# The first heads of a hybrid mLSTM and band-attention trunk: a pool of their own, and their 57 modulation columns dealt anew

## The chip, the cores and the metric

The kernel runs on one core of a Trainium2 chip. The metric is the device time of one launch in microseconds (us), as the median of several runs. TensorE (PE) multiplies, with its weight loads shown apart as PEld; VectorE (DVE) and ScalarE (ACT) work element by element; GpSimd (POOL) and SyncE (SP) only issue DMAs here.

## What is computed

Two layers work on a sequence of 512 tokens of width 2048. The first is an mLSTM layer with 8 heads, the second a band-attention layer whose keys and values come from the residual stream between the two. Each is a modulated RMSNorm, a mixer, and a gated residual. This study is about the first layer:

```python
mod = sc @ ada_w[l] + ada_b[l]                     # sc = silu(c): 1 x 2048 times 2048 x 6144
shift, scale, gate = ...                           # three rows of 2048
h = modulate(rmsnorm(x, g_pre[l]), shift, scale)
proj = h @ w_in                                    # queries, keys, values, output gates o, branch z, cell gates
qk = silu(causal_conv(proj[..., :A_V0], conv_w, conv_b))
ht = mlstm_chunkwise(q, k, v, log_i, log_f)        # per head: decayed scores times values
y = sigmoid(o) * rmsnorm_per_head(ht) * silu(z)
x = x + gate * rmsnorm(y @ w_out)
```

The second layer does the same with `band_attention_mixer`, and its keys and values are modulated by two further rows (`kv_ada_w`). All inputs and outputs are float32.

## The kernel before

**Products.** A float32 product is made of three: each operand is split into a high part (an ACT cast) and a low part (a DVE subtraction), and PE adds high x high, high x low and low x high (`mm3`). A weight piece `wr` of up to 128x1024 is loaded by SP, cast by ACT and subtracted by DVE (L243) into `wh`, which PE then reads. Three `wr` and three `wh` buffers turn round, so the piece numbered n can't be cast before PE has done with n-3, and can't be loaded before n-3 has been subtracted.

**Columns.** The modulation rows are made without PE: for every 128 of their elements a 128x2048 block `ada` (1024 KB) is loaded and one DVE instruction (L552) multiplies it by silu(c) and sums it into one column of `mod`. Here such a block is called a column. The 32 columns of shift and scale (numbers 0 to 31) are needed at the start, two for each of the 16 input tiles. The others are background work: 57 of them (numbers 32 to 47, 96 to 127 and 48 to 56) are summed by `background(n)`, which sums up to n columns that are loaded and asks POOL for new ones. Three are under way at a time, in two buffers of the pool `ada` and one of `ada1`. An `ada` load waits for the sum that last read its buffer. `paced` orders a sum behind the PE product written before it, which places it but is no wait.

**Stages.** At the start, 41 steps (`first_steps`) go over the 16 input tiles: a step (k,) makes the input tile `h1_k` (DVE L521, ACT L523, DVE L524) and multiplies it with six weight tiles into the six accumulators `ps_lead`; the other steps multiply finished input tiles with the other fourteen weight tiles of head 0 and head 1's queries and keys (`ps_l`), and DVE adds these parts in SBUF (L731). Pieces 0 to 40 are their weights. Then heads follow one after the other:

- Head 0 has its projections but for the values from the start. `conv` turns queries and keys into the convolved `qk` tiles (ACT, three DVE taps at L797, ACT SiLU, split). The cell gates follow (`gates`), a chain of DVE, ACT and PE steps with rows that go to DRAM and come back to all partitions as `nm`; DVE adds the causal mask to it (`nmd`, L956). Then the values `ps_v` (pieces 41 to 48), the scores `ps_s`, and decayed scores times values (`ps_n`).
- Head 1 has its queries and keys from the start too; pieces 49 to 56 are its values, 57 to 72 its `o` and `z`.
- Head 2 (`HALF`) is whole, with pieces from 73. From its `o` and `z` on, and in all later heads, products go in the form with seven products in place of eight, and the background must be over.

The normalisation of a head is made of two rows (`row_out`): sums over partitions, by PE with a matrix of ones (`ps_d`, `ps_q`), go through ACT into a tile `row` and by a POOL DMA to DRAM. `factor` brings them back on 16 partitions, DVE and ACT make one factor per token, and POOL brings it to all partitions (`ssum`). POOL's queue is in order: a load of a row that waits for its store holds the column loads behind it.

**The pool t1.** Three buffers of 128x512 (tag `t`) serve nearly everything short-lived: normalised input, convolution accumulators `cv`, copies `cu` of interleaved rows, decays `e`, `sz`, squares `sq`, and the norm rows. A tile must wait until the third last tile of that pool has been read for the last time.

**Order.** The program is written in the order above; a scheduler at build time orders each engine's instructions by its own estimate of durations, with priorities (`tc.high_priority`), and `pin` keeps those marked in program order.

Of the kernel before, what the change touches and what calls it, by code (L numbers as in the profile page):

```python
# [15 lines left out]
P = 128  # L16
# [171 lines left out]
def hybrid_trunk(ctx, tc, xT, xN, c, adaT, cols, wst, wg, ext, kc, out):  # L188
# [132 lines left out]

    def proj(mat, xs, pss, nk, k0, k1, last, t0=0, t1=S, first=None):

        g = len(pss)
        for ka in range(k0, k1, nk):
            [(hi, lo)] = wpiece(mat)
            for k in range(ka, ka + nk):
                x = xs(k) if callable(xs) else xs[k]
                for i, ps in enumerate(pss):
                    w = slice(((k - ka) * g + i) * P, ((k - ka) * g + i + 1) * P)  # L330
                    mm3(ps, hi[:, w], lo[:, w], x[:, 0, t0:t1], x[:, 1, t0:t1], k == (k0 if first is None else first), k == last, S)

    def proj_a(mat, xs, ps, t0=0, t1=S):
        proj(mat, xs, [ps], 8, 0, len(xs), len(xs) - 1, t0, t1)

# [339 lines left out]
    pending = [2 * KT + i for i in range(KT)] + [96 + i for i in range(32)] + [48 + i for i in range(SHIFTS)]  # L675
    loaded = []

# [5 lines left out]
    def background(n):  # L683

        for a in loaded[:n]:
            ada_sum(*a, paced)
        del loaded[:n]
        while pending and len(loaded) < 3:
            p, bufs = (bp, 1) if len(pending) % 3 == 1 else (ap_, 2)
            loaded.append(ada_load(pending.pop(0), p, bufs, pin, queue=nc.gpsimd))  # L690

    due = []
    for n, step in enumerate(steps):
        if n > len(steps) - 6:
            background(2 if n % 2 else 0)
# [36 lines left out]
    st.close()  # L732
    ahead[0] = AHEAD

    hp = hst.enter_context(pool("head"))
# [11 lines left out]
    def gates():  # L747
        g_ps = newa("ps_g")
        for k in range(KT):
            for i in range(2):  # L750
                mm(bank(g_ps[:32], S), gw[:, k, :], walk(h1[k][:, i, :], S), k == 0 and i == 0, k == KT - 1 and i == 1)
        g32 = tp.tile([P, S], F32, tag="t", name="g32")
        nc.scalar.copy(like(g32[:32], S), read(g_ps[:32], S))
# [32 lines left out]

    def conv(ps, ch, name, lead, woven):

        acc = tp.tile([P, S], F32, tag="t", name=f"cv_{name}")
        with tc.high_priority(lead):  # L790
            if woven:
                rows = tp.tile([P, S], F32, tag="t", name=f"cu_{name}")
                nc.scalar.copy(like(rows, S), read(ps, S))
                ps = rows
# [88 lines left out]
    def row_out(h, i, ps, f):  # L883

        r = tp.tile([P, S], F32, tag="t", name=f"row{h}_{i}")[0:1]
        nc.scalar.activation(like(r, S), read(ps[0:1], S), f)
        nc.gpsimd.dma_start(dsc[h, i : i + 1], r)
# [33 lines left out]
    for h in range(NH):  # L921
# [4 lines left out]
        for i in range(4):  # L926
            if h > HALF:
                if i % 2 == 0:
                    zs = pair((i // 2) * (V0 // 2) + h * DK, f"zq{h}_{i}", BANKS[i // 2], HEAD_PAIRS, {1: head_due} if i else {}, lead=AHEAD - 30 * i)
                ps = zs[i % 2]  # L930
            elif h < 2:
                ps = (lead, qk1)[h][i]
            else:
                ps = newp(f"ps_qk{h}_{i}")
                proj_a("a_w_in", h1, ps)
            qk.append(conv(ps, chs[i], f"{h}_{i}", AHEAD if h == HALF else 100 if h > HALF and i > 1 else 0, h in (0, HALF)))
            if 1 < h <= HALF:
                background(2)
                if i in (2, 3):
                    head_due()  # L940
# [7 lines left out]
        if h == 0:  # L948
            background(2)
            gates()  # L950
# [48 lines left out]
        if h < HALF:  # L999
            background(2 + (h == 0))  # L1000
        if h:
            so = []
        for i in range(4):
# [7 lines left out]
            elif h:  # L1011
                ps = newp(f"ps_o{h}_{i}")
                proj_a("a_w_in", h1, ps)
                so.append(acp.tile([P, S], F32, tag="so", name=f"so{h}_{i}", bufs=6))
                nc.scalar.activation(like(so[i], S), read(ps, S), AF.Sigmoid)
                background(2)
        for i in range(4):
            if h >= HALF:
                break
            if h:  # L1020
                ps = newp(f"ps_z{h}_{i}")
                proj_a("a_w_in", h1, ps)
            else:
# [4 lines left out]
            if h and i < 3:  # L1028
                background(2)
        if h == 0:  # L1030
            background(2)
        if h == NH - 1:
# [36 lines left out]
        if h < HALF:  # L1069
            background(3)  # L1070
        if h == 3:
# [637 lines left out]
```

## Time and profile before

| what | value |
|---|---|
| median of 3 runs | 2637.78 us (2635.75 to 2638.52) |
| profiled execution | 2635.22 us |
| its span in the profile | 2633.4 us |
| PE busy | 2574.4 us (98%), 17994 products |
| DVE busy | 2335.1 us (89%) |
| DMA, share of 16 engines, 300 to 400 us | 0.84 |

The views that the prediction shows are these. The waits view gives for an engine and line: who was waited for, the us in total, how often, and the longest. The timeline gives start us, duration us, engine, line, operation, out<-in, shape, how many, and in brackets the idle time before with what ended it. A window row gives, for a stretch, the busy us of PE, PEld, DVE, ACT and POOL with instruction counts, the granted PE clock, the share of the DMA engines and GB/s. A DMA row gives the issues of a line in a stretch, the KB of each, and the median us from issue to landing. Neighbouring rows of one engine overlap a little, so a duration in a row is taken from start to start.

### The profile page before, as it was taken

How to read it: one execution, taken by the hardware profiler on the slowest of the kernel's cores; microseconds unless marked ns; L12 is line 12 of the kernel's file. 1: busy time of each engine (PE TensorE's matmuls, PEld its weight loads, DVE VectorE, ACT ScalarE, POOL GpSimd, SP SyncE). 2: the span in 40 equal slices, each digit the busy share in tenths (PEclk: the TensorE clock that was granted, in tenths of full speed). 3: DMA queues.
4: the chain of work that ended last, by engine and by line, in shares of the span. 5: the costliest groups of instructions: out<-in, count | busy, mean ns of one | idle time of the engine just before them, and what ended most of it. 6: DMA issues, size and time to landing. Idle time of an engine off the chain costs nothing.

```text
span 2633.4 us, 45758 instructions
## 1 busy us (share of the span) xinstructions
PE 2574.4 (98%) x17994; PEld 2407.5 (91%) x17994; DVE 2335.1 (89%) x3812; ACT 1428.7 (54%) x2106; POOL 59.8 (2%) x118
## 2 busy tenths in 40 slices
PE   8999999999999999999999999999999999999998
PEld 6887787899999999999999898788999899999887
DVE  8978988999989999899998886977997999999767
ACT  4344533466555665556655453578543766776523
POOL 0000111000000000000000000000000000000000
PEclk9999999999999999999999999999999999999999
DMA  9876787533333333333336548988654544444787
GB/s 364 313 265 251 272 329 290 192 108 114 124 102 129 115 111 125 105 125 118 110 130 237 195 150 327 301 259 302 226 179 146 171 130 138 138 130 132 254 299 251
DMA packets 155315, 510.62 MB, mean 194 GB/s; under 512 B 17893, under 2 KB 31749, under 8 KB 140633
## 3 DMA queue, kind: packets, MB, share of 16 engines
q1 hardware_dynamic: 144346, 443.89, 49.6%
q0 software_dynamic: 10752, 63.79, 6.6%
q8 instruction: 141, 2.31, 0.4%
q14 instruction: 76, 0.62, 0.1%
HBM read 473.96 MB, written 38.90 MB: 195 GB/s over the span
## 4 chain that ended last, share of the span: by engine, by line
PE 56%; DVE 25%; DMA 8%; issue 7%; ACT 3%; POOL 0%; SPq 0%; DVEq 0%; ACTq 0%; POOLq 0%
DVE wh L243 6%; PE ps_y L311 5%; PE ps_azo L311 4%; PE ps_czo L311 4%; PE ps_dzo L311 4%; DVE ada L552 3%; PE ps_y_True L311 3%; PE ps_dz L311 3%; PE ps_cz L311 3%; PE ps_y_False L311 3%; PE ps_az L311 3%; DMA wr<-in_wst 3%; DVE wsh L243 2%; PE ps_bzo L311 2%; DVE cv L797 2%
## 5 line engine op out<-in xcount | busy, mean ns | idle before, releaser
L243 ACT CAST wh<-wr 128x1024 fp32r<-128x1024 f32 (+1 forms) x536 | 553.3, 1034 | 473.3 <-DVE wr L283 102.0
L243 DVE TENSOR_TENSOR wh<-wr,wh 128x1024 fp32r<-128x1024 f32 (+1 forms) x536 | 643.3, 1203 | 127.2 <-ACT wh L243 126.3
L243 ACT CAST wsh<-ws 128x768 fp32r<-128x768 f32 (+1 forms) x296 | 241.8, 817 | 298.4 <-PE ps_az L311 67.1
L243 DVE TENSOR_TENSOR wsh<-ws,wsh 128x768 fp32r<-128x768 f32 (+1 forms) x296 | 276.8, 935 | 45.7 <-ACT wsh L243 44.5
L552 DVE CUSTOM_DVE_ANT_0 ada<-ada,scB,cl 128x2048 f32<-128x2048 f32 (+1 forms) x89 | 205.8, 2322 | 11.3 <-DMA ada<-in_adaT 11.2
L282 DVE TENSOR_TENSOR ws<-wr 128x512 f32<-128x512 f32 (+1 forms) x296 | 198.5, 673 | 5.3 <-DMA wr<-in_wst 5.0
L311 PE MATMUL ps_y_False<-wh,y 128*128 128x512 f32 x768 | 168.6, 380 | 2.3 <-DVE wh L243 2.2
L311 PE MATMUL ps_y<-wh,y 128*128 128x512 f32 x768 | 168.6, 380 | 0.1
L311 PEld LDWEIGHTS ps_y_False<-wh,y 128*128 128x128 f32 x768 | 144.3, 189 | 24.4 <-DVE wh L243 4.2
L311 PEld LDWEIGHTS ps_y<-wh,y 128*128 128x128 f32 x768 | 144.3, 189 | 20.8 <-DVE wh L243 0.5
L311 PE MATMUL ps_kv<-wh,hkv 128*128 128x512 f32 x576 | 127.3, 381 | 1.6 <-DVE wh L243 1.5
L311 PE MATMUL ps_v<-wh,h 128*128 128x512 f32 x576 | 127.3, 380 | 0.0
L311 PEld LDWEIGHTS ps_kv<-wh,hkv 128*128 128x128 f32 x576 | 108.0, 189 | 18.5 <-DVE wh L243 3.3
L284 DVE TENSOR_TENSOR ws<-wr 128x256 f32<-128x256 f32 (+1 forms) x296 | 122.1, 414 | 3.1
L283 DVE TENSOR_TENSOR wr<-ws,wr 128x256 f32<-128x256 f32 (+1 forms) x296 | 121.8, 413 | 2.4
L311 PEld LDWEIGHTS ps_v<-wh,h 128*128 128x128 f32 x576 | 108.3, 189 | 15.8 <-issue 0.9
L311 PE MATMUL ps_l<-h,wh 128*128 128x512 f32 x480 | 107.7, 380 | 2.1 <-DVE wh L243 2.1
L311 PEld LDWEIGHTS ps_l<-h,wh 128*128 128x128 f32 x480 | 90.3, 189 | 16.5 <-DVE wh L243 3.3
L311 PE MATMUL ps_azo<-h,wh 128*128 128x256 f32 (+1 forms) x606 | 92.9, 285 | 0.0
L311 PE MATMUL ps_y_True<-wh,y 128*128 128x512 f32 x384 | 83.3, 379 | 0.0
L311 PEld LDWEIGHTS ps_y_True<-wh,y 128*128 128x128 f32 x384 | 72.5, 189 | 10.2
L311 PEld LDWEIGHTS ps_azo<-h,wh 128*128 128x128 f32 x606 | 79.2, 192 | 1.1
(431 smaller groups left out, 5825.2 us busy)
## 6 DMA issues: line engine op xcount, KB each, us to landing
wr<-in_wst SPq DMA_DIRECT2D x506, 512.0 KB, 3.7
ada<-in_adaT POOLq DMA_DIRECT2D x57, 1024.0 KB, 7.1
ada<-in_adaT SPq DMA_DIRECT2D x49, 1024.0 KB, 7.0
ada<-in_adaT SPq DMA_DIRECT2D x36, 512.0 KB, 6.5
wr<-in_wst SPq DMA_DIRECT2D x26, 384.0 KB, 6.2
xt<-nsc SPq DMA_DIRECT2D x32, 256.0 KB, 3.8
yr<-ysc SPq DMA_DIRECT2D x28, 256.0 KB, 5.4
ysc<-zo SPq DMA_DIRECT2D x24, 256.0 KB, 3.9
```

The lines of the kernel that those rows point to most:

```text
L243: ins = nc.scalar.copy(hi, src), nc.vector.tensor_tensor(lo, src, hi.bitcast(F32), op=ALU.subtract)
L282: nc.vector.tensor_tensor(t[:, : 2 * w], r[:, w : 3 * w], r[:, : 2 * w], op=ALU.subtract)
L283: nc.vector.tensor_tensor(r[:, w : 2 * w], t[:, w : 2 * w], r[:, :w], op=ALU.add)
L284: nc.vector.tensor_tensor(t[:, 2 * w :], r[:, 3 * w :], r[:, w : 2 * w], op=ALU.subtract)
L311: product[0] = nc.tensor.matmul(ps, a, b, start=start, stop=stop)
L552: pin(nc.vector.tensor_tensor_reduce(c, c, (sc or scB)[:, j * w : (j + 1) * w], 1.0, mod[:, i : i + 1] if j else col(CB + i), ALU.mult, AL ...
L797: nc.vector.scalar_tensor_tensor(acc[:, d:], ps[:, : S - d], col(CW + 32 * (3 - d) + ch), acc[:, d:], op0=ALU.mult, op1=ALU.add)
```

## The change

- A new pool `t0` beside `t1`: convolution accumulators of heads 0 to 2 (three buffers), copies and the gates' `g32` (two), norm rows of heads 0 and 1 (two). It also holds a fourth buffer for columns, from the end of the start on.
- The 57 background columns are dealt anew: summing begins 13 steps before the end of the start in place of 5; after that fewer are asked for at each place, and places in the middle of the projections of head 1 and head 2 are added (`mid`).
- Head 0's mask addition is written behind its values in place of ahead of them.
- The copies of the attention bias (`bsc`, two per head, DRAM to DRAM by SP) move from all eight heads to heads 3 to 7.

```diff
-    def proj(mat, xs, pss, nk, k0, k1, last, t0=0, t1=S, first=None):
+    def proj(mat, xs, pss, nk, k0, k1, last, t0=0, t1=S, first=None, mid=None):
         for ka in range(k0, k1, nk):
+            if mid and ka > k0:
+                mid()
...
-    loaded = []
+    loaded, ring = [], [(ap_, 2), (ap_, 2), (bp, 1)]
...
-        while pending and len(loaded) < 3:
-            p, bufs = (bp, 1) if len(pending) % 3 == 1 else (ap_, 2)
+        while pending and len(loaded) < len(ring):
+            p, bufs = ring.pop(0)
+            ring.append((p, bufs))
...
-        if n > len(steps) - 6:
+        if n > len(steps) - 14:
             background(2 if n % 2 else 0)
...
+    ep = mst.enter_context(pool("t0", side="right"))
+    ring.insert(0, (ep, 1))
...
+    def early_tile(h, tag, bufs, name):
+        return ep.tile([P, S], F32, tag=tag, name=name, bufs=bufs) if h else tp.tile([P, S], F32, tag="t", name=name)
...
-        acc = tp.tile([P, S], F32, tag="t", name=f"cv_{name}")
+        acc = early_tile(early, "cv", 3, f"cv_{name}")
-                rows = tp.tile([P, S], F32, tag="t", name=f"cu_{name}")
+                rows = early_tile(True, "cu", 2, f"cu_{name}")
...
-        r = tp.tile([P, S], F32, tag="t", name=f"row{h}_{i}")[0:1]
+        r = early_tile(h < HALF, "row", 2, f"row{h}_{i}")[0:1]
...
             if 1 < h <= HALF:
-                background(2)
+                background(1)
...
-        nc.vector.tensor_tensor(
-            nmd, nm.rearrange("p (a b) -> p a b", a=4), maskd.unsqueeze(1).to_broadcast([P, 4, P]), op=ALU.add
-        )
+        if h:
+            masked()
...
-            add_at(at, {k: lambda: background(2) for k in (0, 4, 8)})
+            add_at(at, {k: lambda: background(1) for k in (4, 8, 12)})
         elif h < HALF:
-            for k in range(0, KT, 2):
+            for k in (0, 2, 4, 8, 12):
...
-        for i in (2 * h, 2 * h + 1):
+        for i in range(BH * (h - HALF - 1) // (NH - HALF - 1), BH * (h - HALF) // (NH - HALF - 1)) if h > HALF else ():
             pin(nc.sync.dma_start(bsc[i], ext[i].partition_broadcast(P)))
         if h == 0:
+            masked()
...
         if h < HALF:
-            background(2 + (h == 0))
+            background(1)
...
-                proj_a("a_w_in", h1, ps)
+                proj_a("a_w_in", h1, ps, lambda: background(1))
...
         if h < HALF:
-            background(3)
+            background(1 + h)
```

How instructions stand on the engines shows at three places. The first is DVE at the end of the start, from the low half of weight piece 30 (`wh30`) on; `ada` rows are columns, `oz0_7` and `q1_0` are the sums of parts in SBUF, and the read of the accumulator behind each column is left out. Before:

```order
L243 TENSOR_TENSOR wh30_1150<-wr30_1068,wh30_1150 128x768
L552 ISA ada31_0_1070,mod_103<-ada31_0_1070,scB_123,cl_100 128x2048
L552 ISA ada15_0_1072,mod_103<-ada15_0_1072,scB_123,cl_100 128x2048
L243 TENSOR_TENSOR wh31_1178<-wr31_1100,wh31_1178 128x768
L521 SCALAR_TENSOR_TENSOR h1t_15_1315<-xt3_145,amul_104,ssum_108 128x512
L731 TENSOR_TENSOR oz0_7_264<-oz0_7_264,ps_l5_6_1158 128x512
```

Now:

```order
L243 TENSOR_TENSOR wh30_1162<-wr30_1068,wh30_1162 128x768
L554 ISA ada31_0_1070,mod_103<-ada31_0_1070,scB_123,cl_100 128x2048
L554 ISA ada32_0_1122,mod_103<-ada32_0_1122,scB_123,cl_100 128x2048
L554 ISA ada15_0_1072,mod_103<-ada15_0_1072,scB_123,cl_100 128x2048
L734 TENSOR_TENSOR oz0_7_264<-oz0_7_264,ps_l5_6_1170 128x512
L554 ISA ada33_0_1124,mod_103<-ada33_0_1124,scB_123,cl_100 128x2048
L243 TENSOR_TENSOR wh31_1190<-wr31_1100,wh31_1190 128x768
L734 TENSOR_TENSOR q1_0_265<-q1_0_265,ps_l6_6_1195 128x512
L554 ISA ada34_0_1126,mod_103<-ada34_0_1126,scB_123,cl_100 128x2048
L243 TENSOR_TENSOR wh32_1221<-wr32_1131,wh32_1221 128x768
L554 ISA ada35_0_1158,mod_103<-ada35_0_1158,scB_123,cl_100 128x2048
```

Columns 32 and 33 now stand ahead of piece 31, and the first step of the last input tile (`h1t_15`), which stood behind piece 31, now comes between pieces 35 and 36. Up to piece 38 there are ten columns of the background where there were none.

The second place is PE at the scores of head 1 (`ps_s1`, of the query halves `qk_1_0`, `qk_1_1` and the key halves `qk_1_2`, `qk_1_3`). Before, they stood in the first output-gate product, behind all values:

```order
L311 MATMUL ps_v1_3_2132<-wh56_2434,h1_15_1314 128x512 x3
L311 MATMUL ps_o1_0_2480<-h1_0_269,wh57_2483 128x512 x3
L311 MATMUL ps_s1_0_2272<-qk_1_0_2095,qk_1_2_2113 128x512 x2
L311 MATMUL ps_s1_1_2326<-qk_1_0_2095,qk_1_2_2113 128x384 x2
L311 MATMUL ps_s1_2_2373<-qk_1_0_2095,qk_1_2_2113 128x256 x2
```

Now they stand in the values, at piece 53:

```order
L311 MATMUL ps_s1_0_2266<-qk_1_0_2092,qk_1_2_2110 128x512
L311 MATMUL ps_v1_1_2127<-wh53_2290,h1_9_833 128x512 x3
L311 MATMUL ps_v1_2_2128<-wh53_2290,h1_9_833 128x512 x3
L311 MATMUL ps_v1_3_2129<-wh53_2290,h1_9_833 128x512 x2
L311 MATMUL ps_s1_0_2266<-qk_1_1_2101,qk_1_3_2119 128x512 x2
L311 MATMUL ps_v1_3_2129<-wh53_2290,h1_9_833 128x512
L311 MATMUL ps_s1_1_2317<-qk_1_0_2092,qk_1_2_2110 128x384 x3
```

They moved ahead by nearly four pieces. The third place is DVE there, now: the low halves of the keys that these scores read, and a column between them.

```order
L243 TENSOR_TENSOR wh55_2381<-wr55_2379,wh55_2381 128x1024
L805 SCALAR_TENSOR_TENSOR cv_1_3_2113<-q1_3_268,cl_100,cv_1_3_2113 128x509
L243 TENSOR_TENSOR qk_1_2_2110<-cv_1_2_2104,qk_1_2_2110 128x512
L243 TENSOR_TENSOR qk_1_1_2101<-cv_1_1_2095,qk_1_1_2101 128x512
L907 SCALAR_TENSOR_TENSOR f0_2079<-f0_2079 16x32
L554 ISA ada101_0_2084,mod_103<-ada101_0_2084,scB_123,cl_100 128x2048
L243 TENSOR_TENSOR qk_1_3_2119<-cv_1_3_2113,qk_1_3_2119 128x512
```

Column 101 stands ahead of the last key half. On POOL its load stands behind the two norm rows of head 0 and their way back, each of which waits for the store before it:

```order
L895 DMA dsc_73<-row0_0_2008 16x1x32
L901 DMA f0_2079<-dsc_73 16x32
L895 DMA dsc_73<-row0_1_2076 16x1x32
L901 DMA f0_2079<-dsc_73 16x32
L548 DMA ada101_0_2084<-in_adaT 128x2048
```

More of the change, by code (lines that the diff above doesn't have):

```diff
@@ L331, in proj, with proj_a @@
                     mm3(ps, hi[:, w], lo[:, w], x[:, 0, t0:t1], x[:, 1, t0:t1], k == (k0 if first is None else first), k == last, S)
-    def proj_a(mat, xs, ps, t0=0, t1=S):
-        proj(mat, xs, [ps], 8, 0, len(xs), len(xs) - 1, t0, t1)
+    def proj_a(mat, xs, ps, mid):
+        proj(mat, xs, [ps], 8, 0, len(xs), len(xs) - 1, mid=mid)
     def proj_b(mat, xs, pss, ms=range(4), kts=KT, at={}, late=0):
@@ L751, in gates @@
                 mm(bank(g_ps[:32], S), gw[:, k, :], walk(h1[k][:, i, :], S), k == 0 and i == 0, k == KT - 1 and i == 1)
-        g32 = tp.tile([P, S], F32, tag="t", name="g32")
+        g32 = early_tile(True, "cu", 2, "g32")
         nc.scalar.copy(like(g32[:32], S), read(g_ps[:32], S))
@@ L785, in hybrid_trunk, with conv @@
     silu = [None]
-    def conv(ps, ch, name, lead, woven):
-        acc = tp.tile([P, S], F32, tag="t", name=f"cv_{name}")
+    def early_tile(h, tag, bufs, name):
+        return ep.tile([P, S], F32, tag=tag, name=name, bufs=bufs) if h else tp.tile([P, S], F32, tag="t", name=name)
+    def conv(ps, ch, name, lead, woven, early):
+        acc = early_tile(early, "cv", 3, f"cv_{name}")
         with tc.high_priority(lead):
             if woven:
-                rows = tp.tile([P, S], F32, tag="t", name=f"cu_{name}")
+                rows = early_tile(True, "cu", 2, f"cu_{name}")
                 nc.scalar.copy(like(rows, S), read(ps, S))
@@ L934, in hybrid_trunk @@
                 ps = newp(f"ps_qk{h}_{i}")
-                proj_a("a_w_in", h1, ps)
-            qk.append(conv(ps, chs[i], f"{h}_{i}", AHEAD if h == HALF else 100 if h > HALF and i > 1 else 0, h in (0, HALF)))
+                proj_a("a_w_in", h1, ps, lambda: background(1))
+            qk.append(conv(ps, chs[i], f"{h}_{i}", AHEAD if h == HALF else 100 if h > HALF and i > 1 else 0, h in (0, HALF), h <= HALF))
             if 1 < h <= HALF:
-                background(2)
+                background(1)
                 if i in (2, 3):
@@ L948, in hybrid_trunk @@
         if h == 0:
-            background(2)
+            background(1)
             gates()
@@ L955, in hybrid_trunk, with masked @@
         nc.sync.dma_start(nm, gsc[0, h].partition_broadcast(P))
-        nc.vector.tensor_tensor(
-            nmd, nm.rearrange("p (a b) -> p a b", a=4), maskd.unsqueeze(1).to_broadcast([P, 4, P]), op=ALU.add
-        )
+        def masked():
+            nc.vector.tensor_tensor(
+                nmd, nm.rearrange("p (a b) -> p a b", a=4), maskd.unsqueeze(1).to_broadcast([P, 4, P]), op=ALU.add
+            )
+        if h:
+            masked()
         pr, tot = [], []
@@ L999, in hybrid_trunk @@
         if h < HALF:
-            background(2 + (h == 0))
+            background(1)
         if h:
@@ L1012, in hybrid_trunk @@
                 ps = newp(f"ps_o{h}_{i}")
-                proj_a("a_w_in", h1, ps)
+                proj_a("a_w_in", h1, ps, lambda: background(1))
                 so.append(acp.tile([P, S], F32, tag="so", name=f"so{h}_{i}", bufs=6))
@@ L1021, in hybrid_trunk @@
                 ps = newp(f"ps_z{h}_{i}")
-                proj_a("a_w_in", h1, ps)
+                proj_a("a_w_in", h1, ps, lambda: background(1))
             else:
@@ L1029, in hybrid_trunk @@
                 background(2)
-        if h == 0:
-            background(2)
         if h == NH - 1:
```

## The prediction, made before the changed kernel was run

> **What bounds the kernel now.** I read the head of the page first, then PE's waits, then windows, the timeline of each wait in the stretch that the change touches, and the DMA rows behind them. The page:
>
> ```profile
> span 2633.4 us, 45758 instructions
> PE 2574.4 (98%) x17994; PEld 2407.5 (91%) x17994; DVE 2335.1 (89%) x3812; ACT 1428.7 (54%) x2106; POOL 59.8 (2%) x118
> ```
>
> PE is the bound: all its idle time is 59 us, and the change leaves its products alone. So the change is worth the PE stalls that it takes away, less those it makes, nearly one for one at the end. PE's waits in the whole kernel (us in total, times, longest), those of the first heads:
>
> ```profile
> PE ps_q L311 <- ACT sp_q L243: 4.9, 5, 3.8
> PE ps_s L311 <- ACT qk L243: 4.4, 1, 4.4
> PE ps_z L311 <- DVE wh L243: 3.4, 2, 2.7
> PE ps_n L311 <- DVE so L1054: 1.3, 1, 1.3
> PE ps_bzo L311 <- DVE p L872: 0.7, 1, 0.7
> ```
>
> The places, from PE's timeline, and what was late for the 3.81, from ACT's:
>
> ```profile
> 229.41 0.38 PE L782 MATMUL ps_at<-kcs,ssum 8*128 8x8 f32 x4 [1.24 <-DVE ssum L773]
> 315.09 2.21 PE L311 MATMUL ps_s<-qk,qk 128*128 128x512 f32 x6 [4.37 <-ACT qk L243]
> 385.27 15.81 PE L311 MATMUL ps_z<-h,wh 128*128 128x512 f32 x72 [2.68 <-DVE wh L243]
> 422.90 0.48 PE L311 MATMUL ps_q<-sp_q,ones_r 128*128 128x512 f32 x1 [3.81 <-ACT sp_q L243]
> ```
>
> ```profile
> 420.22 0.60 ACT L1053 ACTIVATE sq<-ps_n 128x512 f32<-128x512 f32 x1 [5.69 <-DMA dsc<-row]
> ```
>
> ACT stood 5.69 us because the square's buffer in `t1` had held a norm row, which is free only when its DMA to DRAM has read it. The windows (busy us of PE, PEld, DVE, ACT, POOL, then granted clock, DMA share, GB/s):
>
> ```profile
> 140.00:160.00 20.00, 20.00 (x95) 17.50 (x94) 17.95 (x24) 7.54 (x11) 1.74 (x3) 1.00 1.02 410
> 160.00:180.00 20.00, 20.00 (x95) 17.50 (x94) 9.68 (x11) 9.37 (x12) 0.00 (x0) 1.00 0.42 136
> 180.00:200.00 20.00, 20.00 (x94) 17.53 (x93) 19.90 (x24) 12.76 (x16) 1.59 (x3) 1.00 0.63 223
> 300.00:320.00 20.00, 15.63 (x67) 13.38 (x66) 20.00 (x26) 10.98 (x15) 1.59 (x3) 0.91 0.81 315
> 400.00:420.00 20.00, 16.61 (x86) 14.01 (x84) 16.38 (x19) 4.61 (x7) 3.11 (x6) 1.00 1.00 393
> 420.00:440.00 20.00, 17.10 (x79) 14.85 (x80) 15.76 (x18) 7.18 (x10) 3.09 (x6) 1.00 0.55 211
> ```
>
> Three things are to be seen: PE never stands from 140 to 200; DVE and the DMA engines lie half empty from 160 to 180; at 300 to 320 DVE is full, and at 400 to 420 the DMA engines are.
>
> **The change part by part.** *The start.* Ten background columns (32 to 41) come ahead of the low half of piece 38 where there were none. PE's steps there, DVE's rows for the durations, and the loads (KB, us to landing, at 150.5, 140.0 and 185.5):
>
> ```profile
> 149.77 11.82 PE L311 MATMUL ps_l<-h,wh 128*128 128x512 f32 x54
> 165.31 7.93 PE L311 MATMUL ps_l<-h,wh 128*128 128x512 f32 x36
> 173.08 4.05 PE L311 MATMUL ps_lead<-h,wh 128*128 128x512 f32 x18
> 176.96 26.06 PE L311 MATMUL ps_l<-h,wh 128*128 128x512 f32 x120
> ```
>
> ```profile
> 115.20 1.82 DVE L243 TENSOR_TENSOR wh<-wr,wh 128x768 fp32r<-128x768 f32 x2
> 116.94 0.74 DVE L521 SCALAR_TENSOR_TENSOR h1t<-xt,amul,ssum 128x512 f32<-128x512 f32 x1
> 117.60 2.34 DVE L552 CUSTOM_DVE_ANT_0 ada<-ada,scB,cl 128x2048 f32<-128x2048 f32 x1
> 147.88 2.35 DVE L552 CUSTOM_DVE_ANT_0 ada<-ada,scB,cl 128x2048 f32<-128x2048 f32 x1
> 185.82 2.34 DVE L552 CUSTOM_DVE_ANT_0 ada<-ada,scB,cl 128x2048 f32<-128x2048 f32 x1
> 188.09 0.69 DVE L731 TENSOR_TENSOR oz<-oz,ps_l 128x512 f32<-128x512 f32 x1
> 188.69 2.35 DVE L243 TENSOR_TENSOR wh<-wr,wh 128x1024 fp32r<-128x1024 f32 x2
> 190.96 0.68 DVE L731 TENSOR_TENSOR oz<-oz,ps_l 128x512 f32<-128x512 f32 x1
> ```
>
> ```profile
> 150.55 1.06 POOL L546 DMA_DIRECT2D ada<-in_adaT  x2 [9.54 <-DVE mod L552]
> ```
>
> ```profile
> ada<-in_adaT POOLq DMA_DIRECT2D x1, 1024.0 KB, 6.8
> ```
>
> ```profile
> ada<-in_adaT POOLq DMA_DIRECT2D x1, 1024.0 KB, 9.5
> ```
>
> ```profile
> ada<-in_adaT POOLq DMA_DIRECT2D x1, 1024.0 KB, 5.1
> ```
>
> From start to start a column takes DVE 2.27 (185.82 to 188.09), a low half 0.87 at 768 wide (115.20 to 116.94, two) and 1.14 at 1024, a sum of parts 0.60, the `h1` steps and a convolution tap 0.66 each. By the new order columns 31, 32 and 15 and a sum of parts go from 147.88 to 155.3. Column 33, whose load can be issued at 150.55 as a column's is now, lands 6.8 later, at 157.35, and is summed at 159.6; piece 31's low half is done at 160.5. PE wants that half at 149.77 + 38 products of 0.216 = 158.0: a stall of 2.5, where there is none now. From 159.6 to the end of piece 38's low half DVE has eight columns (18.2), five halves of 768 (4.4) and three of 1024 (3.4), eight sums of parts (4.8), two taps, the two steps of `h1_15` and small ones (3.2), and I add 0.8 for casts and a landing that it waits for: 194.4. PE wants that half at 176.96 + 54 x 0.216 = 188.6. The start thus costs 194.4 - 188.6 = **5.8**, felt as 2.5 at piece 31, about 0.8 and 0.5 at `h1_15` (its first step ends at 175.6, ACT's cast at 176.5, PE wants it at 173.08 + 2.6) and 2.0 at piece 38. The two bounds: were the column landings all 5.1, as at share 0.63, column 33 would be there at 155.7, 1.6 sooner, and the cost 4.2; were they all 9.5, as at share 1.02, 2.7 later, and 8.5.
>
> *Bandwidth around head 1's `o` and `z`.* From piece 60 to 68 there are 12 columns and 8 pieces, 16.8 MB, in eight pieces of 24 products, 41.4 us: 405 GB/s, where the row at 400 shows 393 moved at share 1.00. PE is then late by about 1.3; three buffers of weights cover half of that: **+0.7**.
>
> *The gate chain* keeps its 1.24 and gets a column more in DVE's way on one of its links: **+0.2**. *Norm rows of head 0*, whose PE steps now follow each other more closely: **+0.4** (nothing to 1).
>
> *Head 1's scores.* Before, PE met them at 310.7, and the last key half came at 315.09. The rows that set it:
>
> ```profile
> 301.99 2.07 DVE L797 SCALAR_TENSOR_TENSOR cv<-q,cl,cv 128x511 f32<-128x511 f32 x3
> 291.67 0.49 POOL L893 DMA_DIRECT2D f<-dsc  x1 [7.75 <-DMA dsc<-row]
> 294.23 0.49 POOL L893 DMA_DIRECT2D f<-dsc  x1 [1.58 <-DMA dsc<-row]
> ```
>
> Now the taps need no buffer of `t1` and stand earlier on DVE, so the 4.37 goes, and with it the halved clock behind it. The window at 300 grants 0.91 over 20 us, that is 20 x 0.09 = 1.8 lost, of which I take 1.7: **-6.1**. The scores stand four pieces earlier now, though, at piece 53, and the last key half stands on DVE behind column 101, whose load stands on POOL behind row trips like the 7.75. My estimate is that column 101 lands when DVE wants it or up to 3 us later: **+1.3** (nothing to 10; see the third rival). The Trainium skill, page "TensorE: Matmul & The Clock Gate", section "Part 1: The HAM clock gate (the "warmup" mystery)", says that the array's clock halves after an idle window of about 3.4 us and comes back after about 3.4 us of work, the window running freely. By it the 3.81 could cost 1.7 as well, and the sum would be lower by that; the trace shows it for the 4.37 alone (0.91 against 1.00 at 420).
>
> *Head 1's `z`.* The 2.68 and the other 0.7 come where columns and weights ask for more than the full DMA engines give. Columns are taken out of the way of the first `z` weights by the fourth one under way, which lets DVE work ahead, but by the order 25 are summed between pieces 57 and 76 before and after, so some stays: I let 3.4 become 0.6, **-2.8** (0 to -3.4).
>
> *Head 1's end.* With rows in `t0` the square waits for no row DMA, and the 3.81 goes, with 1.3 at `ps_n` whose operand was late on the same chain; 0.3 is kept: **-4.8** (-3.8 to -5.1). *Head 2's first numerators*, 0.7 on DVE's `p`: **-0.8** with fewer columns there.
>
> The busy tenths of the DMA engines in the page's 40 slices of 66 us:
>
> ```profile
> DMA  9876787533333333333336548988654544444787
> ```
>
> The mask order and the `bsc` copies cost nothing: the copies go from the first eight slices to heads 3 to 7, in the row of threes that begins with the ninth, and the mask waits for nothing that PE needs sooner. If that cover were missing it would be 0.7 of DVE, one addition.
>
> Sum: 5.8 + 0.7 + 0.2 + 0.4 + 1.3 = 8.4 added; 6.1 + 2.8 + 4.8 + 0.8 = 14.5 removed; net **-6.1**. The profiled execution, 2635.2 with a span of 2633.4 and 1.8 around it, lies 2.6 under the median; it would become 2629.1, and the median 2637.8 becomes **2631.7**.
>
> **The rivals.** *First: DVE absorbs the start.* DVE is idle 10.3 us from 160 to 180 and the pieces have three buffers, so the stalls after piece 31 could vanish, leaving 2.5 of 5.8 and all else as it is: -6.1 - 3.3 = -9.4, **2628.4**. Against it: the ten columns are 22.7 us and the idle time of DVE from 150 to 180 is 12.
>
> *Second: the dealing does not relieve the full DMA engines.* The number of columns between pieces 57 and 76 stays at 25, a fourth in flight only takes landing time from the weights, so `z` keeps its 3.4 and 1.0 of the norm stays: -6.1 + 2.8 + 1.0 = -2.3, **2635.5**, no change to be measured. For it: a landing takes 9.5 at share 1.02 and 5.1 at 0.63. The Trainium skill, page "DMA: Bandwidth & Descriptors", section "Issuing engines are not separate DMA queues", says that transfers started by whichever engine run on the same 16 DMA engines and interleave; the trace agrees with these two landings. Against it: the window 420 to 440 is at 0.55, and PE's stall there was not a load.
>
> *Third, slower: head 1's keys wait behind column 101.* If the first row trip on POOL lasts its 7.75 again and the load behind it 9.5, column 101 lands at 305 to 310, where DVE wants it, by my working of the order, at about 299; the last key half then comes 6 to 11 late, with a halved clock (1.8) behind it, in place of my 1.3. The kernel is then at -7.4 + 7.8 = +0.4 to -7.4 + 12.8 = +5.4. If the second trip, 1.58 here, lasts 7.75 too, 6.2 more come on top, +11.6; the middle of the whole is +6, **2644**. It decides against the old kernel from a wait of 5.6 with the clock on top. For it: the long trip is in this very place, at a DMA share of 0.81. Against it: the second trip was short, and the new dealing asks for fewer columns ahead of it.
>
> **How the numbers follow.** Forecast 0.54, first rival 0.10, second 0.20, third 0.16. A measurement of this kernel can tell about 0.2%, 5.3 us, from no change, so faster means under 2632.5 and slower over 2643.1. The forecast's own spread is -3 to -9, from the bounds of the start (4.2 to 8.5) and of `z`; it is faster in 0.38 of its 0.54, no change in the other 0.16. With the first rival faster is 0.48. The second is all no change, and the third is 0.06 no change and 0.10 slower: no change 0.16 + 0.20 + 0.06 = 0.42, slower 0.10. The range reaches from 2626.5, near where the first rival stands with the landings of 5.1 (-9.4 - 1.6), to 2641.0, over the second rival and into the third; it leaves out the third's upper half (0.10) and a thin end of the forecast and the first rival (0.05).
>
> **What would show it.** Right: `ps_s` of head 1 with a wait under 3 us and clock 1.00 behind it; no `row` release in front of `sq` at head 1's end, and `ps_q` under 0.5; stalls of 2 to 3 at piece 31 and again at piece 38 in the stretch 155 to 200 that has none now, DVE there without idle time. Wrong: no PE idle time from 150 to 200 (first rival); `ps_z` with 3 us or more and a DMA share of 1.00 from 380 to 420 (second); column 101 with a wait of over 5 us on DVE and `ps_s` stalled (third). A stall over 3 us at head 0's norm or in the gates, which I price at 0.6 together, would break the sum.

## The result, and the profile after

The changed kernel takes 2623.06 us (median of 7 runs, 2620.04 to 2630.82) where the one before takes 2637.78; the ratio is 0.9947, interval 0.9932 to 0.9963, so 14 us are gone (10 to 18). Beside the experiments it was timed twice more, on other chips, with 0.9943 both times (0.9928 to 0.9957 and 0.9929 to 0.9957). The profiled execution takes 2621.64, with a span of 2619.9 in place of 2633.4. The forecast was 2631.7, its range 2626.5 to 2641.0: the direction was right, but the time lies 3.4 us below the range, and the gain is more than twice the forecast 6.1.

PE's waits after, as in the view shown of before:

```profile
PE ps_l L311 <- DVE wh L243: 4.8, 5, 2.3
PE ps_at L787 <- DVE ssum L778: 1.6, 1, 1.6
PE ps_l L311 <- DVE oz L734: 1.2, 2, 1.0
PE ps_q L311 <- ACT sp_q L243: 1.1, 4, 0.3
PE ps_s L311 <- DVE qk L243: 0.2, 1, 0.2
```

`ps_q` (4.9) and `ps_s` (4.4) are nearly gone, `ps_z` and `ps_n` (3.4 and 1.3) have no row left, and `ps_l`, the start, has taken their place (2.1 before, 4.8 and 1.2 now). The windows answer to those of before:

```profile
140.00:160.00 20.00, 18.10 (x84) 15.50 (x82) 17.97 (x19) 6.18 (x9) 2.48 (x5) 1.00 1.01 410
160.00:180.00 20.00, 19.62 (x82) 16.60 (x83) 18.61 (x20) 4.38 (x5) 2.37 (x5) 0.91 0.94 358
180.00:200.00 20.00, 17.77 (x79) 14.34 (x78) 19.29 (x25) 9.22 (x13) 2.11 (x4) 1.00 0.83 310
300.00:320.00 20.00, 19.81 (x98) 17.23 (x98) 11.99 (x18) 11.14 (x15) 2.62 (x5) 1.00 0.79 278
400.00:420.00 20.00, 20.00 (x105) 17.72 (x104) 18.06 (x22) 6.95 (x11) 3.81 (x8) 1.00 0.73 292
420.00:440.00 20.00, 20.00 (x94) 17.50 (x94) 20.00 (x29) 9.49 (x13) 2.12 (x4) 1.00 0.76 287
```

PE now stands 4.5 us from 140 to 200 and runs at 0.91 there; from 400 to 440, where it stood 6.3, it does not stand at all. Where the 13.5 us of span went is read by setting the same places of the program side by side. First the gates' product `ps_g` in the tile view of before and of after (last come the starts of the first and the last of the 32):

```profile
L311 PE MATMUL ps_g<-h,gw x32: 379/379/379, 202.9 to 209.6; 128*32 128x512 f32 x32
```

```profile
L311 PE MATMUL ps_g<-h,gw x32: 379/379/379, 210.6 to 217.3; 128*32 128x512 f32 x32
```

Then the places behind it in PE's timeline, of before and of after:

```profile
361.28 21.32 PE L311 MATMUL ps_z<-h,wh 128*128 128x512 f32 x98
462.37 20.88 PE L311 MATMUL ps_v<-wh,h 128*128 128x512 f32 x96
645.62 0.49 PE L311 MATMUL ps_cv<-wsh,h1s 128*128 128x256 f32 x2 [1.56 <-DVE wsh L243]
2094.68 0.79 PE L311 MATMUL ps_dz<-h2s,wh 128*128 128x256 f32 x2 [1.77 <-DVE h2s L243]
2593.94 0.27 PE L825 MATMUL ps_gg<-kcs,ggate 128*4 128x128 f32 x1 [1.60 <-DVE ggate L823]
```

```profile
362.77 41.60 PE L311 MATMUL ps_z<-h,wh 128*128 128x512 f32 x192
453.72 20.88 PE L311 MATMUL ps_v<-wh,h 128*128 128x512 f32 x96
635.97 0.49 PE L311 MATMUL ps_cv<-wsh,h1s 128*128 128x256 f32 x2 [1.56 <-DVE wsh L243]
2083.83 0.49 PE L311 MATMUL ps_dz<-h2s,wh 128*128 128x256 f32 x2 [1.67 <-DVE h2s L243]
2580.27 0.27 PE L833 MATMUL ps_gg<-kcs,ggate 128*4 128x128 f32 x1 [1.49 <-DVE ggate L831]
```

| stretch of the program | after less before, at its end | of the stretch | the prediction's terms |
|---|---|---|---|
| the start, to `ps_g` | +7.7 | +7.7 | +5.8 |
| heads 0 and 1, to head 1's `z` | +1.5 | -6.2 | -6.1 + 0.2 + 0.4 + 1.3 = -4.2 |
| head 1's `z`, its end, head 2's queries and keys | -8.7 | -10.1 | +0.7 - 2.8 - 4.8 = -6.9 |
| the rest of head 2, into head 3 | -9.7 | -1.0 | -0.8 |
| heads 3 to 7, layer 2 up to `ps_dz` | -10.9 | -1.2 | 0 |
| from there to the end | -13.7 | -2.8 | 0 |

(At the very end 0.2 come back.) The last row is no shorter work and no wait (PE stands 1.7 us in that stretch before and 1.6 after): it is TensorE's clock. In before, two waits of 1.68 and 1.77 at `ps_dz` are followed by a halved clock, shown by windows of 3 and 4 us; after has one wait of 1.67 there and the clock stays whole. The wait of 1.68 that is gone is more than all of the row above, -1.2. The first two rows are of before, the third of after:

```profile
2093.00:2096.00 3.00, 1.32 (x6) 1.32 (x7) 3.00 (x7) 1.17 (x2) 0.00 (x0) 0.59 0.51 159
2096.00:2100.00 4.00, 4.00 (x21) 4.00 (x21) 3.95 (x7) 0.46 (x2) 0.00 (x0) 0.50 0.15 45
```

```profile
2096.00:2100.00 4.00, 4.00 (x36) 3.92 (x35) 3.93 (x8) 2.75 (x3) 0.00 (x0) 1.00 0.46 153
```

At `ps_dz` this is in part the luck of the two executions that are compared. In another profiled execution of the very same changed kernel (the one that stands beside the pair of pool and fourth column below), waits of 0.65 and 1.77 stand there, and the clock is halved behind them:

```profile
2082.68 0.60 PE L311 MATMUL ps_dz<-h2s,wh 128*128 128x256 f32 x2 [1.77 <-DVE h2s L243]
```

```profile
2084.00:2087.00 3.00, 3.00 (x19) 3.00 (x19) 3.00 (x5) 0.45 (x2) 0.00 (x0) 0.61 0.03 10
```

So the last two rows of the table can't be credited to the change. Over all runs there is a difference, wherever in the program it arises: the granted clock averages 0.9962 over the 83 runs of before that stand beside the experiments and 0.9979 over the 18 runs of the changed kernel. 0.0017 of 2637 us is about 4.5 us, by this estimate a third of the gain.

### The profile page after: what moved, and what is told of

Read it like the earlier page. It is cut to its first block, busy times and chain, and to the rows that moved or that the text cites. A ratio compares the mean times of both kernels' runs of the same rounds, so it can differ in the third digit from the quotient of the medians.

```text
span 2619.9 us, 45758 instructions
## 1 busy us (share of the span) xinstructions
PE 2571.5 (98%) x17994; PEld 2404.1 (92%) x17994; DVE 2334.8 (89%) x3812; ACT 1423.9 (54%) x2103; POOL 59.5 (2%) x118
## 5 line engine op out<-in xcount | busy, mean ns | idle before, releaser
L311 PEld LDWEIGHTS ps_v<-wh,h 128*128 128x128 f32 x576 | 108.2, 189 | 15.8 <-issue 0.9
```

Of the source, the lines that this page charges most:

```text
L311: product[0] = nc.tensor.matmul(ps, a, b, start=start, stop=stop)
```

## The experiments

The change has three parts that can be had singly: the pool, the fourth column and the dealing. Times are medians; ratios are to the kernel before, timed beside it on the same chip, and kernels of different chips are compared by their ratios.

**The pool alone.** Convolutions, copies, `g32` and the rows of heads 0 and 1 go to a pool `t0`, on the kernel before:

```diff
+    ep = mst.enter_context(pool("t0", side="right"))
...
-        acc = tp.tile([P, S], F32, tag="t", name=f"cv_{name}")
+        acc = early_tile(early, "cv", 3, f"cv_{name}")
...
-        r = tp.tile([P, S], F32, tag="t", name=f"row{h}_{i}")[0:1]
+        r = early_tile(h < HALF, "row", 2, f"row{h}_{i}")[0:1]
```

> The kernel before with the pool for convolutions, copies and norm rows alone; columns dealt as before, three under way. Theory (the pool takes away the waits at head 1's scores and at its end, the dealing those at z, and the dealing's early columns cost the start): no stall at ps_s and ps_q of head 1, ps_z keeps about 3.4, no stall from 150 to 200, in all about -11 us against before, 2626 to 2628. Rival (the dealing takes all of them away, since head 1's keys and rows are late because DVE and the DMA engines are full of columns): the pool alone is worth 3 us or less, 2634 or more, with ps_s still waiting 3 us or more.

2626.16, ratio 0.9952 (0.9938 to 0.9967), -13 us. The theory holds for the pool: `ps_s` of head 1 waits 1.16 in place of 4.37, its `ps_q` not at all, and the full stretch, from 340 to 400 at a DMA share of 0.99 to 1.00, keeps its stalls (5.3 in four places, the fourth one 0.43):

```profile
307.65 0.75 PE L311 MATMUL ps_s<-qk,qk 128*128 128x512 f32 x3 [1.16 <-DVE qk L243]
355.95 5.02 PE L311 MATMUL ps_o<-h,wh 128*128 128x512 f32 x22 [1.51 <-DVE wh L243]
373.11 10.63 PE L311 MATMUL ps_z<-h,wh 128*128 128x512 f32 x48 [1.34 <-DVE wh L243]
391.61 15.38 PE L311 MATMUL ps_z<-h,wh 128*128 128x512 f32 x70 [2.00 <-DVE wh L243]
```

**All but the pool.** The changed kernel, with those tiles back in `t1`:

```diff
-        acc = early_tile(early, "cv", 3, f"cv_{name}")
+        acc = tp.tile([P, S], F32, tag="t", name=f"cv_{name}")
...
-        r = early_tile(h < HALF, "row", 2, f"row{h}_{i}")[0:1]
+        r = tp.tile([P, S], F32, tag="t", name=f"row{h}_{i}")[0:1]
```

> The changed kernel with convolutions, copies and norm rows back in the old pool; its dealing, the fourth column, the mask and the bias copies as changed. Theory: the start costs its 7.7 us (stalls and halved clock), ps_z has no stall, head 1's scores and its end wait 4 to 5 us each: +3 to +6 against before, about 2642. Rival (the dealing is what helps): -8 or better against before, 2630 or less.

2628.32, ratio 0.9961 (0.9947 to 0.9976), -10 us. My theory had +3 to +6, and it fell: without the pool `ps_s` waits 1.06 and 2.61 and `ps_q` is free. So dealing and fourth column take away the same waits as the pool, and the parts don't add.

**The rows alone.** Only the norm rows of heads 0 and 1 leave `t1`:

```diff
+    ep = mst.enter_context(pool("t0", side="right"))
...
-        r = tp.tile([P, S], F32, tag="t", name=f"row{h}_{i}")[0:1]
+        r = (ep.tile([P, S], F32, tag="row", name=f"row{h}_{i}", bufs=2) if h < HALF else tp.tile(...))[0:1]
```

> The kernel before with the norm rows of heads 0 and 1 in buffers of their own, nothing else. Theory: the 3.81 at ps_q goes with 1 us of ps_n, the 4.37 at ps_s and its clock stay, z stays: -4 to -5 us, about 2634. Rival (the row's trip to DRAM on full DMA engines holds something else up): within 2 us of before, the stall under another name.

2630.59, ratio 0.9956 (0.9944 to 0.9969), -11.5 us: more than twice the theory's. The 4.37 at `ps_s` goes too, to 0.90, although the convolutions are still in `t1`. So head 1's keys had been late for the reason that head 1's end was late: a row, held until its DMA to DRAM was done, blocked the buffer of a convolution. ACT of before shows it, the convolution's first instruction waiting for the row (the row's trip of 7.75 on POOL ends at 291.67):

```profile
293.79 0.81 ACT L795 ACTIVATE cv<-q,cl 128x512 f32<-128x512 f32 x1 [1.57 <-DMA dsc<-row]
```

At the scores, the two kernels with the dealing and the old pool come to the same end in another way. There the same row's trip is 1.83 (all but the pool) and 1.64 (the dealing alone, below), not 7.75. In before, POOL issues two column loads in the 4 us ahead of that row; in these two the last one stands 5 us ahead, which is the likely reason, though no run tried it alone:

```profile
281.48 0.49 POOL L901 DMA_DIRECT2D f<-dsc  x1 [1.83 <-DMA dsc<-row]
```

```profile
280.16 0.49 POOL L896 DMA_DIRECT2D f<-dsc  x1 [1.64 <-DMA dsc<-row]
```

At head 1's end this does not explain it: the row's trip in all but the pool is 8.02 there, as long as the 7.78 of before, and yet no square waits for its buffer. Why not stays open.

**Mask and bias copies alone**, on the kernel before:

```diff
-        for i in (2 * h, 2 * h + 1):
+        for i in range(BH * (h - HALF - 1) // (NH - HALF - 1), ...) if h > HALF else ():
...
         if h == 0:
+            masked()
```

> The kernel before with head 0's mask addition behind its values and the bias copies in heads 3 to 7, nothing else. Theory: nothing of the gain is from these two: within 2 us of before, 2636 to 2641. Rival (the copies' DMA time in the first heads, or DVE's wait of 3.5 us for nm ahead of the mask, holds the columns up): -3 us or more, with shorter waits at ps_s or ps_z.

2639.28 against 2642.04, ratio 0.9993 (0.9983 to 1.0003): no gain that can be told from nothing, as the theory has it. `ps_s` waits 3.12 and `ps_q` 3.08, each about 1 less than in before; whether that is theirs was not tried further.

**The start begun late.** The changed kernel with the background 5 steps ahead of the start's end:

```diff
-        if n > len(steps) - 14:
+        if n > len(steps) - 6:
```

> The changed kernel with the background begun 5 steps before the end of the start, as before the change, in place of 13. Theory: the start's 7.7 us come back (no PE stall from 155 to 200, no halved clock there); the eight columns that are then left over at head 2 fall where DVE has little to spare, and cost 0 to 5 there: 2616 to 2621, 2 to 8 us under the changed kernel. Rival (the columns summed at the start are what keeps z free): ps_z stalls 3 us or more and the whole is as slow as the changed kernel or slower, 2623 or more.

2634.47, ratio 0.9983 (0.9973 to 0.9992): by the ratios about 10 us worse than the changed kernel, and not by either theory. The start is free and so is `z`; what costs is the eight columns left over, which DVE sums one after another in head 2, ahead of the decays `e`, with 3.4 us more lost to a halved clock at each of the two stalls:

```profile
498.00 1.62 PE L311 MATMUL ps_s<-qk,qk 128*128 128x256 f32 x6 [8.18 <-DVE e L875]
509.64 0.98 PE L311 MATMUL ps_azo<-h,wh 128*128 128x256 f32 x3 [5.42 <-DVE e L875]
```

The direction of the price was right, its size (0 to 5) was not.

**Three columns under way.** The changed kernel without the fourth buffer:

```diff
-    ring.insert(0, (ep, 1))
```

> The changed kernel with three columns under way in place of four. Theory (the fourth matters little, since the DMA engines are full from 340 to 400 either way): within 2 us of the changed kernel, 2621 to 2625. Rival (the fourth lets DVE work ahead of the full stretch and is what took z's stall away): ps_z stalls 2 us or more, 2626 or more.

2635.33, ratio 0.9986 (0.9977 to 0.9994): by the ratios about 11 us worse than the changed kernel. The rival is right that the fourth matters, but not at `ps_z`, where PE does not wait at all here: PE stands 3.24 at `ps_n` of head 1 and 1.88 in head 2, and its clock is halved five times ahead of the program's end (at the start for twice as long), the changed kernel's once. What the fourth does is seen in the full stretch, first this kernel, then the changed one:

```profile
340.00:360.00 20.00, 20.00 (x94) 17.53 (x93) 14.28 (x14) 5.18 (x6) 2.64 (x5) 1.00 0.93 359
360.00:380.00 20.00, 20.00 (x95) 17.50 (x94) 16.31 (x16) 6.58 (x7) 2.64 (x5) 1.00 0.93 360
```

```profile
340.00:360.00 20.00, 20.00 (x95) 17.50 (x94) 18.40 (x16) 5.19 (x6) 3.17 (x6) 1.00 1.00 403
360.00:380.00 20.00, 20.00 (x94) 17.53 (x93) 17.66 (x16) 6.57 (x7) 2.89 (x6) 1.00 1.01 416
```

403 and 416 GB/s in place of 360 (from 380 to 400 three reach 399 too): over the whole program DVE waits 28.7 us for columns with three, with four 15.8.

**The fourth column alone**, on the kernel before, and **the dealing alone** (the changed kernel without pool and fourth):

```diff
+    loaded, ring = [], [(ap_, 2), (ap_, 2), (bp, 1)]
...
-        while pending and len(loaded) < 3:
+        while pending and len(loaded) < len(ring):
...
+    ring.insert(0, (ep, 1))
```

The edit shown is that of the first of the two.

> The kernel before with a fourth column under way and nothing else: old pool, old dealing. Theory (the fourth keeps the DMA engines full from 340 to 400, 416 GB/s in place of 360, so that DVE gets its columns sooner and the full stretch ends sooner): ps_z has 1 us of stall or less in place of 3.4 and ps_n's 1.8 go; ps_s and ps_q keep 3 to 4 each; -4 to -8 us against before. Rival (it only interleaves with the weights' loads, since the engines are full already): within 2 us of before, or slower, with ps_z at 3 us or more.

> The changed kernel without its pool and without the fourth column: the dealing, the mask and the bias copies alone. Theory (the dealing shortens the rows' way to DRAM, so ps_s and ps_q are nearly free, but pays the start's 7.7 and, with three columns, stalls of 3 and 2 us behind the full stretch): as the changed kernel with three columns or 2 to 4 slower, 0 to -4 us against before. Rival (without the pool the dealing brings nothing and costs the start): 6 us or more slower than before.

The fourth alone: 2632.99, ratio 0.9981 (0.9971 to 0.9992), -5 us. `ps_z` falls from 3.4 to 1.2 and `ps_s` keeps 4.18, as the theory has it; against it, `ps_n` keeps 2.0 and `ps_q` falls to 1.43. The dealing alone: 2635.56, ratio 0.9991 (0.9981 to 1.0002), -2 us; `ps_s` waits 0.64, the start is crowded, and behind the full stretch stand 1.87 and 3.26 at `ps_n`, as its theory has it.

**Pool and fourth column, old dealing**, the pair that was left, with the changed kernel beside it:

```diff
+    ep = mst.enter_context(pool("t0", side="right"))
+    ring.insert(0, (ep, 1))
...
```

> The kernel before with the new pool and the fourth column, its old dealing, mask and bias copies. Theory (the waits at ps_s and ps_q go with the rows' own buffers, the waits at ps_z and ps_n with the fourth column, and the dealing only adds the start's cost): no stall over 2 us from 200 to 520, none from 140 to 200, -16 to -22 us against before, under the changed kernel. Rival (the dealing is needed besides, since the old one sums too many columns around head 1's keys or too few by head 2): -10 to -14 us, with stalls of 3 us or more at ps_s, ps_z or in head 2.

> The changed kernel beside it on one chip: -13 to -15 us against before.

2620.23 (2617.49 to 2623.47), ratio 0.9931 (0.9918 to 0.9944), -18 us; the changed kernel beside it 2623.12 (2621.18 to 2625.65), ratio 0.9943. By the medians it is 3 us ahead, but the intervals overlap. No stall over 2.1 us from 200 to 520, none from 140 to 200, as the theory has it. The dealing as it stands thus adds nothing to the other two (the mask order and the bias copies go with it in this table; above they were worth nothing). The parts together:

| pool | fourth | dealing | ratio | us (ratio less 1, times 2639) |
|---|---|---|---|---|
| x | | | 0.9952 | -13 |
| | x | | 0.9981 | -5 |
| | | x | 0.9991 | -2 |
| x | x | | 0.9931 | -18 |
| | x | x | 0.9961 | -10 |
| x | | x | 0.9986 | -4 |
| x | x | x | 0.9943 | -15 |

By the medians, which leave each difference uncertain by some 5 us, the pool is worth 13 without the dealing and 1 to 5 with it: these two take away the same waits. The fourth column and the dealing are the other way round: the fourth is worth 5 with the old dealing and 8 to 11 with the new.

**A start begun 4 steps later**, and **the same with its four columns spread** over the values of heads 0 and 1:

```diff
-        if n > len(steps) - 14:
+        if n > len(steps) - 10:
...
-            add_at(at, {k: lambda: background(1) for k in (4, 8, 12)})
+            add_at(at, {k: lambda: background(1) for k in (4, 8, 10, 12, 14)})
...
-            for k in (0, 2, 4, 8, 12):
+            for k in (0, 2, 4, 6, 8, 10, 12):
```

The first has the first of these three edits only.

> The changed kernel with its background begun 9 steps before the end of the start in place of 13, so that no column stands ahead of pieces 31 to 34; four columns fewer are summed by head 2's output gates, and are summed there in a row. Theory (what the changed kernel loses is DVE time at the start, and what the late start lost, 8.2 and 5.4 us at head 2, grows with the number left over): the start's 7.7 us shrink to 2 or less, head 2's stall is 3 to 7 us with a halved clock behind it; 2619 to 2626, as the changed kernel or slightly better. Rival (a handful of leftovers costs nothing): 2616.

> As the one before, but with the four columns put into the values of head 0 and head 1 (two more places each), where the changed kernel's DVE is idle 5 to 8 us in 20 and the DMA share is 0.4 to 0.8; from piece 60 on it has summed as many as the changed kernel. Theory: no stall over 1 us at the start, none at head 2, ps_z and head 1's end free: 6 to 8 us under the changed kernel, 2614 to 2618. Rival (DVE or POOL is too late for head 1's keys there, or the gates, so the cost only moves): 2621 or more, with a stall at ps_at, ps_n or ps_s of over 3 us.

The first: 2619.12, ratio 0.9915 (0.9902 to 0.9928). The start's stalls are gone, as the theory has it; the stall in head 2 that I expected is not there, so four leftovers cost next to nothing where eight made stalls of 13.6. The time lies at the edge of what the theory gave, 2619, but not for its reason. The second: 2614.9 and, on another chip, 2615.43, ratios 0.9900 (0.9885 to 0.9916) and 0.9921 (0.9905 to 0.9938), where the changed kernel beside the latter has 0.9943. It is the fastest here, 8 us under the changed kernel, and its start shows why:

```profile
140.00:160.00 20.00, 20.00 (x95) 17.50 (x94) 18.27 (x23) 7.23 (x11) 1.70 (x3) 1.00 1.02 407
160.00:180.00 20.00, 20.00 (x94) 17.53 (x93) 15.76 (x16) 9.48 (x12) 2.12 (x4) 1.00 0.68 251
180.00:200.00 20.00, 20.00 (x94) 17.50 (x94) 20.00 (x23) 9.21 (x11) 1.60 (x3) 1.00 0.85 309
```

PE never stands there: DVE sums columns in the 160 to 180 that it had idle, and no background column ahead of piece 31.

**The spread kernel again, with the old pool, and with three columns**, beside the changed kernel (the edits are those above):

> The changed kernel, unchanged, so that it stands beside the next three on one chip. 2620 to 2626, -14 us against before; a PE stall of 2 to 3 at piece 31, with or without a halved clock behind it.

> The changed kernel with the background begun four steps later and the four columns spread over the values of heads 0 and 1, again. If its gain is real: 6 to 10 us under the changed kernel beside it, no stall over 1 us from 150 to 200. If it was the chip of that call: within 3 us of it.

> The spread kernel with convolutions, copies and norm rows back in the old pool. Theory (both the pool and the dealing free the same waits, the one by giving the rows their own buffers, the other by shortening the rows' way to DRAM, so with the dealing the pool is worth what it was in the changed kernel, about 5 us): 4 to 7 us over the spread kernel, with stalls of 1 to 3 us at head 1's scores. Rival (with columns back in the values of head 0 and 1 the row's trip is long again, and the rows in the old pool bring back 4 us at ps_s and 4 at ps_q): 10 us or more over it.

> The spread kernel with three columns under way. Theory (with three the columns come late to DVE in the places where it has time, and PE waits at head 1's end, 3.2 in the changed kernel with three): 5 to 12 us over the spread kernel, a stall at ps_n of head 1. Rival (the fourth was needed only because the start was crowded): within 2 us of it.

The changed kernel 2623.22, the spread one 2615.43, with the old pool 2615.43 (ratio 0.9919, 0.9904 to 0.9933), with three columns 2627.86 (0.9964, 0.9950 to 0.9977). The theory on the pool fell, and its rival too: with this dealing the pool is worth nothing. The rows' trips are 1.92 and 3.00 at head 0's end, where a convolution waits 1.04 for one, and 8.29 at head 1's end, where no tile waits for it. The theory on the fourth column holds, at the upper end: 12 us, with 4.49 at `ps_n` of head 1 and a halved clock behind it:

```profile
409.73 3.42 PE L311 MATMUL ps_n<-p,v 128*128 128x512 f32 x11 [4.49 <-DVE so L1065]
```

## Why the prediction was wrong

Two steps of the prediction failed: the price of head 1's `z` and end, with a term for bandwidth that has the wrong sign, and everything behind head 2, which the prediction put at nothing. At head 1's scores a cost of 1.3 hardly came. The start was priced too low, which hid a part of all this.

**The start** was right in mechanism and place, 5.8 forecast and 7.7 measured. The stalls came as written: 2.25 at piece 31 (2.5 forecast), 0.57 at `h1_15`, 1.02 and 0.44 around piece 38, in all 4.5; at piece 38 it is less than the 2 to 3 that the signs had. What I left out is the clock: I counted none, and behind the 2.25 it is halved. Sixteen products take 5.41 there and 3.72 in the kernel without the pool, where the clock stays whole (both rows stand at the end of this document), so 1.7 us are lost. That leaves 1.5 that are no wait in the profile. The same sixteen products are 3.46 by my 0.216 a product and 3.72 in the row, so a break costs some 0.25 more than its wait; five waits make 1.3 of it, an estimate. The Trainium skill, page "TensorE: Matmul & The Clock Gate", section "Part 1: The HAM clock gate (the "warmup" mystery)", has the clock halve after an idle window of about 3.4 us. Here a wait of 2.25 did it, and the measurement decides. The first rival is out: PE stands 4.5 us there.

**Head 1's scores**: -6.1 forecast for the 4.37 and its clock, and that came. The +1.3 for the keys behind column 101 came as 0.2. Of the +0.6 for gates and rows, the gates took 0.4 (1.64 in place of 1.24), but head 0's norm lost the 0.52 that it waited in before. The row trip on POOL, 7.75 before, was 1.46 in the changed kernel, and DVE does not wait for column 101; so the third rival had its queue right and its trip wrong:

```profile
281.19 0.49 POOL L901 DMA_DIRECT2D f<-dsc  x1 [1.46 <-DMA dsc<-row]
```

I had priced the fewer columns ahead of it as an argument only, with no number. The reason I gave, that the taps "need no buffer of `t1`", is too wide: moving the rows alone took the wait down to 0.90, with the taps still in `t1`.

**Head 1's `z` and end** is the first step that failed, -6.9 forecast and -10.1 measured. The +0.7 for bandwidth has the wrong sign: I took 393 GB/s at share 1.00 as the engines' limit and 405 as more than they could do, and they moved 403 and 416. My own windows of before had said so: the row at 140 shows 410. A share near 1.00 is no fixed rate in these runs: before moves 363 GB/s at 0.99 from 340 to 360, the changed kernel 403 at 1.00. `z` lost all of its 3.4, not 2.8. Bandwidth alone is not the reason: with the new dealing and three columns `ps_z` does not wait either, and with the fourth alone it still waits 1.2. I kept 0.3 at the end where nothing stayed, and left out a wait of 0.47 at `ps_n` for the row on ACT that went too. The remaining 1.2 is again no wait but what five breaks cost beside their waits, 9.0 us in all before and none after. The end is not freed by the rows' pool alone, as I had it: with the pool and the dealing but three columns, `ps_n` waits 3.24 there.

The second rival fell on the bandwidth too. The sentence of the Trainium skill, page "DMA: Bandwidth & Descriptors", section "Issuing engines are not separate DMA queues", on which it draws says that all transfers run on the same engines. That a fourth one brings no bandwidth was my own conclusion, and 360 against 416 GB/s from 360 to 380 refutes it: with three under way the engines were not quite full there (share 0.93), since a new load is only asked for when DVE is through with a column.

**Head 2**, -0.8 forecast and -1.0 measured, was right by luck. The 0.73 on `p` went as forecast, but 0.78 at `ps_czo` came in its place. What makes the number is the second 1.3 at `ps_n` (L1054, operand `zo`), which stood in the same view of before and is gone from the changed kernel; I had counted only that of `so`:

```profile
592.50 3.75 PE L311 MATMUL ps_n<-p,v 128*128 128x512 f32 x22 [1.27 <-DVE zo L1054]
```

**Behind it** is the second step that failed: I had nothing, and 4 us came, 2.8 of clock behind `ps_dz` and 1.2 ahead of it, where the wait of 1.68 is gone. No edit but the bias copies reaches these stages. At `ps_dz` another execution of the changed kernel halves the clock as well, so this part is at least partly luck, and its cause stays open. That the changed kernel runs at a higher clock over all is not: 0.9962 and 0.9979 are means of all runs. That fewer stalls leave fewer places for the clock to halve is an argument, which no run tried alone.

In all the sum missed 7.5 us of the profiled execution: +1.9 at the start, -2.0 at the scores, -3.2 at `z` and head 1's end, -0.2 in head 2, -4.0 behind it. Without the start's miss it would have been 9.4.

## What to carry to other kernels

Two parts of a change that take away the same wait by different means don't add, and can each stand in for the other, so price them as a pair, as the pool and the dealing here. Two parts can also be worth more together than singly, as the dealing and the fourth column seem to be. A small tile that leaves by DMA should not share a rotating pool with tiles on the critical path: with the DMA engines busy it held its buffer for nearly 8 us here. (It need not cost anything: with the spread dealing the rows in `t1` do not.) And background work is best put where the view shows the engine idle: columns from ahead of piece 31 on cost the start 8 us, and with the first behind piece 34 they cost it nothing.

## What the runs showed of the hardware

The clock halves behind waits of 1 to 3 us, but not always. The first row is of the changed kernel, the second of the one without the pool, in the same place:

```profile
160.35 5.41 PE L311 MATMUL ps_l<-h,wh 128*128 128x512 f32 x16 [2.25 <-DVE wh L243]
```

```profile
160.44 3.72 PE L311 MATMUL ps_l<-h,wh 128*128 128x512 f32 x16 [2.44 <-DVE wh L243]
```

The longer wait kept the clock whole. The difference of the rows is 1.7 us; at half speed that is a stretch of 3.4 us. With three columns and a wait of 2.91 in that place it lasted twice as long:

```profile
160.86 6.75 PE L311 MATMUL ps_l<-h,wh 128*128 128x512 f32 x16 [2.91 <-DVE wh L243]
```

In the kernel begun 4 steps later a wait of 0.93, among a few small products of the gates, was enough:

```profile
211.65 1.02 PE L311 MATMUL ps_li<-g,kcs 32*8 32x512 f32 x2 [0.93 <-ACT g L758]
```

```profile
212.00:214.00 2.00, 2.00 (x5) 0.39 (x4) 2.00 (x4) 1.36 (x3) 0.00 (x0) 0.77 0.02 8
214.00:216.00 2.00, 2.00 (x5) 1.62 (x6) 2.00 (x3) 1.95 (x4) 0.00 (x0) 0.50 0.00 0
```

In the spread kernel the same wait, 0.93 at 211.57, left the clock at 1.00, and a wait of 1.53 at 131 us never halved it in the eighteen profiled executions. A stall of PE of about 1 to 3 us is thus to be priced at itself, some 0.25 for the break and a chance of 1.7 for the clock.
